# 32 bytes behind each 512-column block of the first half's operand tiles, and 96 bytes between the rings of high and low weight parts

## The chip, the cores and the metric

The kernel runs on one core of one Trainium2 chip. The metric is device time in microseconds of that core; lower is better.

## The reference

Two transformer-like blocks over a sequence of 1024 tokens with a width of 1024, in float32, one after the other.

```python
# first block
h = rmsnorm(x, g_mix); proj = h @ w_in            # q, k, v of three attentions, 3 gates
o_swa, o_dsa, o_mem = sliding window, top-256 sparse, memory cross attention
merged = sum(sigmoid(gate_i) * (o_i @ w_proj_i))
x = x + merged @ w_out
x = x + square(relu(rmsnorm(x, g_mlp) @ w_mlp_in)) @ w_mlp_out      # 4096 hidden
x = rmsnorm(x, g_final)
# second block, modulated by c: mod = silu(c) @ w_ada + b_ada
h = rmsnorm(x, g_mix_2) * (1 + sc1) + sh1
x = x + gt1 * mixer(h)                            # two-way mLSTM (4 heads) and pooling
h = rmsnorm(x, g_ffn_2) * (1 + sc2) + sh2
x = x + gt2 * (square(relu(h @ w_ff1)) @ w_ff2)
return rmsnorm(x, g_final_2)
```

## The kernel before, in words

Every large product is made of three matmuls in fp32r: each float32 operand is split in a high part (the value rounded to fp32r) and a low part (what is left), and hi x hi, hi x lo and lo x hi are accumulated in the same PSUM bank.

*Weights.* `wunit` (lines 135 to 138) takes a tile of high parts (`wh`) and one of low parts (`wl`) from two rings of three tiles each in the pool `wp`, and `wload` (128 to 133) lets SyncE load the float32 weights into a third ring (`wr`, two tiles), ScalarE round them into `wh` (L131) and VectorE or GpSimd write the rest to `wl` (L132). A tile of the rings has 4096 bytes in each partition, mostly eight blocks of 128 columns (512 bytes each). `gates_ahead` uses rings of its own (`fh`, `fl`, in the pool `fwp`) in the same way.

*Activations.* The 1024 tokens are worked in two halves (hf 0 and 1) of 512. `h_tiles` (152 and 153) makes, for one half, a tile of high and one of low parts, each with eight blocks (one for 128 of the 1024 features) of 512 columns, 2048 bytes to a block. The first half's tiles are in pool `hA`, the second half's in `hB`, or in `hBp` in the first block's MLP and in the second block's mixer. They are written block by block in `norm_turn` (L177, L178) and `make_h` (L1077 to L1081). The hidden layer of the MLPs (`hid_hi`, `hid_lo`, pool `hidp`), the merged product (`m_hi`, `m_lo`), the attention outputs (`o_s`, `om`, `od`) and the mixer's output (`y_s`) are held in the same way, in tiles of their own.

*The order on TensorE.* `gemm_T` (410 on) goes over the feature blocks c and, for each, over the halves. Each (c, half) is one trio: L419 streams the high part of the activations against the block of `wh`, L420 the low part against the same block, L421 the high part against the block of `wl`. `gemm2` (L1303 to L1305) and `gates_ahead` (L269 to L271) have the same trio. Each matmul has a weight load of its own, which runs while the matmul before it streams: beside L419 the `wh` block is loaded again (for L420), beside L420 the `wl` block (for L421), beside L421 the next `wh` block. Attention and the mLSTM use narrower matmuls and transposes; between these `fill` and `fill2` put single trios of the gates or projections. In `gemm_nat` (303 on) the roles are exchanged: the weights stream (256 to 384 columns) and 128 tokens of the activations are stationary.

*Where the tiles lie.* Pools on the left side of the memory grow upwards, those on the right side ("right") downwards from a fixed top; the tiles of a pool lie in ascending order of their first use. In each partition `h_hi` of `hA` begins at byte 21,728, its `h_lo` at 38,112, the pair of `hB` at 54,496 and 70,880, that of `hBp` at 88,032 and 104,416. `hid_hi` begins at 120,800 in the first MLP and 91,616 in the second. `wh` begins at 196,576, `wl` at 208,864, `wr` at 221,152 (it ends 32 bytes below the top of 229,376), and `fh` at 184,288. All of these are 224 more than a multiple of 256, and so are `m_hi`, `m_lo`, `y_s`, `o_s` and `od`. `om`, in a right-hand pool, begins at 161,632 and 169,824: 96 more than a multiple of 256. So do the tiles `m_hi` and `m_lo` of the memory's norm (pool `mT`, 145,504 and 153,696), which are stationary in `gemm_nat`. Three small unused tiles, `offA` (32 bytes), `offB` (768, before `hBp`) and `offC` (256, at the head of the second MLP's `hidp`) set some of these places.

Of the kernel before, what the change touches and what calls it, by code (L numbers as in the profile page):

```python
# [11 lines left out]
F32R = mybir.dt.float32r  # L12
# [7 lines left out]
P = 128  # L20
# [3 lines left out]
DC = D // P  # L24
# [36 lines left out]
def block_kernel(ctx, tc, x, mem, positions, g_mix, w_in, b_gate, sinks, g_mem, w_mem_kv, w_proj_swa, w_proj_dsa,  # L61
# [25 lines left out]
    def raw(ap):  # L87
        return ap.bitcast(F32)

    cst = Pool("cst")  # L90
    wp = Pool("wp", side="right")
# [33 lines left out]
        G.tensor_tensor(dst, dst, mhalf.to_broadcast(list(dst.shape)), op=OP.pow)  # L125


    def wload(src, k0, nk, c0, ncol, hi, lo, eng):
        r = wp([P, nk, ncol], F32, tag="wr", bufs=2)
        nc.sync.dma_start(r, src[k0 * P:(k0 + nk) * P, c0:c0 + ncol].rearrange("(k p) e -> p k e", p=P))  # L130
        A.copy(hi, r)  # L131
        (eng or V).tensor_tensor(lo, r, raw(hi), op=OP.subtract)  # L132
        return hi, lo

    def wunit(src, k0, nk, c0, ncol, eng=None):
        hi = wp([P, nk, ncol], F32R, tag="wh", bufs=3)
        lo = wp([P, nk, ncol], F32R, tag="wl", bufs=3)
        return wload(src, k0, nk, c0, ncol, hi, lo, eng)

# [9 lines left out]
    hA = Pool("hA")  # L149
    hB = Pool("hB")  # L150

    def h_tiles(pool):
        return tuple(pool([P, DC, 512], F32R, tag=f"h_{n}") for n in ("hi", "lo"))

    HT = [h_tiles(hA), h_tiles(hB)]

    def norm_load(pool, src, t):
# [87 lines left out]
    def gates_ahead(todo):  # L245
# [3 lines left out]
        def load(g, i):  # L249
            br, e = g  # L250
            hi = fwp([P, 4, P], F32R, tag="fh", bufs=2)
            lo = fwp([P, 4, P], F32R, tag="fl", bufs=2)
            units[g, i] = wload(w_in[0], 4 * i, 4, C_G + br * D + e * P, P, hi, lo, G)
# [61 lines left out]
    def nat_units(src, c0, ncol):  # L315
        if ncol <= P:
            return [wunit(src, 0, DC, c0, ncol)]
        return [wunit(src, 0, DC // 2, c0, ncol), wunit(src, DC // 2, DC // 2, c0, ncol)]
# [112 lines left out]
    def gate_tanh(br, e, put, eng=None):  # L431

        ug = [wunit(w_in[0], 0, DC, C_G + br * D + e * P, P, eng)]
        ag = [(hf, mm_bank()) for hf in range(2)]
        gemm_T(ag, ug, h_rhs)
        for hf, a in ag:
            A.activation(put(hf), a, AF.Tanh, bias=hbg[:, br * 8 + e:br * 8 + e + 1], scale=0.5)
# [421 lines left out]
    vd = kdp([P, NT, 64], tag="vd")  # L859
    ud = [wunit(w_in[0], k0, 2, C_QD, 384, G) for k0 in (0, 2)]  # L860
    ud += [wload(w_in[0], k0, 2, C_QD, 384, kdp([P, 2, 384], F32R), kdp([P, 2, 384], F32R), G) for k0 in (4, 6)]
    tr = Pool("tr")

# [220 lines left out]
    stp = Pool("stp", side="right")  # L1084
    xtp = Pool("xtp", side="right")
    HT[:] = [h_tiles(hA), None]
    xs = {}

# [19 lines left out]
    hBp = Pool("hBp")  # L1108
    hBp([P, 192], tag="offB")
    HT[1] = h_tiles(hBp)  # L1110


# [101 lines left out]
    hidp = Pool("hidp")  # L1214
# [494 lines left out]


    hidp = Pool("hidp")
    hidp([P, 64], tag="offC")
    ots = {}
    gb_ = hidp([P, D], tag="gb")
    nc.scalar.dma_start(gb_, g_final_2.unsqueeze(0).to_broadcast([P, D]))
# [68 lines left out]
```

## Time and profile before

| what | us |
|---|---|
| median of 2 runs | 2722.95 (2722.44 to 2723.46) |
| the profiled execution | 2722.59 |
| its span | 2720.9 |
| PE busy in the span | 2654.3 |
| VectorE / ScalarE / GpSimd busy | 1440.9 / 919.8 / 342.1 |

The span runs from the first to the last instruction of the program; 1.7 us of the execution lie around it. PE is TensorE. A matmul's record in the profile lasts longer than the step from its start to the next one's start, since matmuls are pipelined: at a step of 226 to 227 ns the record has 389 ns, and a step that is longer by some ns has a record that is longer by as many. The steps are read from the start times in the timeline.

### The profile page before, as it was taken

What the parts mean: (1) busy time and instruction counts of PE and PEld (TensorE: products, weight loads), DVE (VectorE), ACT (ScalarE), POOL (GpSimd) and SP (SyncE); (2) the same over time, 40 slices, a digit from 0 to 9 for tenths busy, and PEclk for the clock granted to TensorE, in tenths of its full rate; (3) what the DMA queues carried; (4) which work ended last, traced back from release to release, by engine and by line L of the source; (5) the groups of instructions that cost most, each with busy time, mean ns of one, the idle gap of its engine ahead of it and who ended that gap; (6) DMA issues with size and microseconds to landing.
All of it is one profiled execution on the core that took longest, in us unless ns stands there. A gap on an engine that the chain in (4) does not pass through costs nothing.

```text
span 2720.9 us, 34328 instructions
## 1 busy us (share of the span) xinstructions
PE 2654.3 (98%) x13328; PEld 2229.8 (82%) x13328; DVE 1440.9 (53%) x2836; ACT 919.8 (34%) x1826; POOL 342.1 (13%) x337
## 2 busy tenths in 40 slices
PE   7999999899999999999999989999999999999997
PEld 6899987788878888888888867888788888888886
DVE  7685878834455634553453476656553333333335
ACT  6575765335334221222212332332432122111223
POOL 3011123421001000000000331111310000000006
PEclk9999999999999999999999999999999999999999
DMA  3121122321154313331331124221421111121123
GB/s 114 53 61 40 31 75 88 93 57 41 63 166 124 108 46 114 116 100 52 108 101 55 57 55 151 63 78 39 139 70 54 57 37 47 51 58 48 39 62 124
DMA packets 263735, 206.41 MB, mean 76 GB/s; under 512 B 9468, under 2 KB 239636, under 8 KB 263572
## 3 DMA queue, kind: packets, MB, share of 16 engines
q1 hardware_dynamic: 255108, 180.25, 22.1%
q10 hardware_dynamic: 8464, 23.96, 2.6%
q8 instruction: 105, 1.72, 0.3%
q14 instruction: 58, 0.48, 0.1%
HBM read 185.24 MB, written 18.94 MB: 75 GB/s over the span
## 4 chain that ended last, share of the span: by engine, by line
PE 70%; DVE 4%; DMA 2%; ACT 1%; issue 1%; POOL 1%; POOLq 0%; SPq 0%; ACTq 0%; DVEq 0%
PE mm L420 19%; PE mm L421 19%; PE mm L419 19%; PE mm L1303 2%; PE mm L1305 2%; PE mm L1304 2%; PE tp L912 1%; DVE st_acc L1007 1%; PE mm L900 1%; DMA adaw<-in_w_ada_dram 1%; DVE h_lo L1081 0%; ACT wh L131 0%; DMA xt<-in_x_dram 0%; DVE t L1074 0%; PE fl L269 0%
## 5 line engine op out<-in xcount | busy, mean ns | idle before, releaser
L131 ACT CAST wh<-wr 128x1024 fp32r<-128x1024 f32 (+3 forms) x303 | 255.1, 843 | 689.2 <-PE mm L420 583.4
L421 PE MATMUL mm<-h_hi,wl 128*128 128x512 f32 x1248 | 486.1, 389 | 1.1 <-POOL wl L132 1.1
L419 PE MATMUL mm<-h_hi,wh 128*128 128x512 f32 x1248 | 486.5, 390 | 0.6 <-ACT ft L278 0.6
L420 PE MATMUL mm<-h_lo,wh 128*128 128x512 f32 x1248 | 485.7, 389 | 0.0
L420 PE MATMUL mm<-hid_lo,wh 128*128 128x512 f32 (+1 forms) x1056 | 405.5, 384 | 4.0 <-DVE hid_lo L1162 4.0
L419 PE MATMUL mm<-hid_hi,wh 128*128 128x512 f32 (+1 forms) x1056 | 407.4, 386 | 0.0
L421 PE MATMUL mm<-hid_hi,wl 128*128 128x512 f32 (+1 forms) x1056 | 405.1, 384 | 0.0
L132 POOL TENSOR_TENSOR wl<-wr,wh 128x1024 fp32r<-128x1024 f32 (+5 forms) x60 | 127.2, 2124 | 1466.8 <-ACT wh L131 1465.1
L1160 DVE TENSOR_TENSOR ml_q<-ml_r 128x512 f32<-128x512 f32 x128 | 88.1, 688 | 419.4 <-ACT ml_r L1158 419.4
L421 PEld LDWEIGHTS mm<-h_hi,wl 128*128 128x128 f32 x1248 | 234.4, 188 | 51.4 <-POOL wl L132 2.0
L419 PEld LDWEIGHTS mm<-h_hi,wh 128*128 128x128 f32 x1248 | 234.4, 188 | 49.7 <-ACT ft L278 0.8
L420 PEld LDWEIGHTS mm<-h_lo,wh 128*128 128x128 f32 x1248 | 234.5, 188 | 48.5
L132 DVE TENSOR_TENSOR wl<-wr,wh 128x1024 fp32r<-128x1024 f32 (+2 forms) x243 | 235.4, 969 | 52.0 <-ACT wh L131 48.5
L420 PEld LDWEIGHTS mm<-hid_lo,wh 128*128 128x128 f32 x1056 | 199.1, 189 | 43.8 <-DVE hid_lo L1162 5.5
L421 PEld LDWEIGHTS mm<-hid_hi,wl 128*128 128x128 f32 x1056 | 199.0, 188 | 39.0
L419 PEld LDWEIGHTS mm<-hid_hi,wh 128*128 128x128 f32 x1056 | 198.9, 188 | 38.5
L1158 ACT ACTIVATE ml_r<-mm 128x512 f32<-128x512 f32 x128 | 76.7, 599 | 449.2 <-PE mm L421 449.2
L1066 DVE SCALAR_TENSOR_TENSOR x<-mm,mod,x 128x512 f32<-128x512 f32 (+1 forms) x152 | 105.7, 722 | 223.0 <-PE mm L421 223.0
L1303 PE MATMUL mm<-h_hi,wh 128*128 128x512 f32 x320 | 131.8, 412 | 0.5 <-DVE kn L1336 0.5
L1305 PE MATMUL mm<-h_hi,wl 128*128 128x512 f32 x320 | 126.9, 396 | 3.3 <-DVE wl L132 3.3
L1304 PE MATMUL mm<-h_lo,wh 128*128 128x512 f32 x320 | 126.2, 394 | 0.0
L1064 DVE TENSOR_TENSOR h_hi<-mm,h_hi 128x512 f32<-128x512 f32 x72 | 49.6, 689 | 125.0 <-PE mm L421 124.9
(474 smaller groups left out, 4579.0 us busy)
## 6 DMA issues: line engine op xcount, KB each, us to landing
adaw<-in_w_ada_dram SPq DMA_DIRECT2D x48, 512.0 KB
wr<-in_w_ff_dram SPq DMA_DIRECT2D x44, 512.0 KB
wr<-in_w_in_dram SPq DMA_DIRECT2D x42, 512.0 KB
wr<-in_w_out_dram SPq DMA_DIRECT2D x32, 512.0 KB
wr<-in_w_mlp_in_dram SPq DMA_DIRECT2D x32, 512.0 KB
wr<-in_w_mlp_out_dram SPq DMA_DIRECT2D x56, 256.0 KB
wr<-in_w_ff_dram SPq DMA_DIRECT2D x56, 256.0 KB
wr<-in_w_in_dram SPq DMA_DIRECT2D x20, 256.0 KB
```

The lines of the kernel that those rows point to most:

```text
L131: A.copy(hi, r)
L132: (eng or V).tensor_tensor(lo, r, raw(hi), op=OP.subtract)
L419: mm(a, hi, r_hi, start=(i == 0), stop=False)
L420: mm(a, hi, r_lo, start=False, stop=False)
L421: mm(a, lo, r_hi, start=False, stop=(i == n - 1))
L1064: V.tensor_tensor(d, a, d, op=OP.add)
L1066: V.scalar_tensor_tensor(d, a, scale[:, e:e + 1], d, op0=OP.mult, op1=OP.add)
L1158: A.activation(r, a, AF.Relu)
L1160: V.tensor_tensor(q, r, r, op=OP.mult)
L1303: mm(a, hi[:, k, :], r_hi, start=(k == 0), stop=False)
L1304: mm(a, hi[:, k, :], r_lo, start=False, stop=False)
L1305: mm(a, lo[:, k, :], r_hi, start=False, stop=(k == DC - 1))
```

## The change

The tiles of `hA` get blocks of 520 instead of 512 columns; the last 8 (32 bytes) of each are never used. A tile of 24 floats (96 bytes) is put into the pool `wp` once, after the first `wh` and before the first `wl`. The 256 bytes of `offC` go.

```diff
+    off_w = []
...
     def wunit(src, k0, nk, c0, ncol, eng=None):
         hi = wp([P, nk, ncol], F32R, tag="wh", bufs=3)
+        if not off_w:
+            off_w.append(wp([P, 24], tag="offW"))
         lo = wp([P, nk, ncol], F32R, tag="wl", bufs=3)
...
     def h_tiles(pool):
-        return tuple(pool([P, DC, 512], F32R, tag=f"h_{n}") for n in ("hi", "lo"))
+        w = 520 if pool is hA else 512
+        return tuple(pool([P, DC, w], F32R, tag=f"h_{n}")[:, :, :512] for n in ("hi", "lo"))
...
     hidp = Pool("hidp")
-    hidp([P, 64], tag="offC")
```

By the layout above, block k of the first half then lies 32 k bytes further on, everything on the left behind `hA` 512 bytes further (256 in the second MLP's `hidp`), and `wh`, with every right-hand pool below `wp`, 96 bytes lower; `wl` and `wr` stay.

## Rows read from the trace of the kernel before

**Rows 1.** The page: busy time by engine, the granted TensorE clock in 40 slices of the span, and the shares of the chain that ended last, by engine and by line.

```profile
PE 2654.3 (98%) x13328; PEld 2229.8 (82%) x13328; DVE 1440.9 (53%) x2836; ACT 919.8 (34%) x1826; POOL 342.1 (13%) x337
...
PEclk9999999999999999999999999999999999999999
...
PE 70%; DVE 4%; DMA 2%; ACT 1%; issue 1%; POOL 1%; POOLq 0%; SPq 0%; ACTq 0%; DVEq 0%
PE mm L420 19%; PE mm L421 19%; PE mm L419 19%; PE mm L1303 2%; PE mm L1305 2%; PE mm L1304 2%; PE tp L912 1%; DVE st_acc L1007 1%; PE mm L900 1%; DMA adaw<-in_w_ada_dram 1%; DVE h_lo L1081 0%; ACT wh L131 0%; DMA xt<-in_x_dram 0%; DVE t L1074 0%; PE fl L269 0%
```

**Rows 2.** Two of the waits of PE for other engines, the first of the list and hid's: total us, times, longest.

```profile
PE tp L1024 <- DVE st_acc L1009: 7.4, 3, 3.8
...
PE mm L420 <- DVE hid_lo L1162: 4.0, 3, 1.7
```

**Rows 3.** Groups of the trio's first matmul with 512 columns, over the whole span, shapes apart: count | busy us, mean ns of a record | idle us before it.

```profile
L419 PE MATMUL mm<-h_hi,wh 128*128 128x512 f32 x1248 | 486.5, 390 | 0.6 <-ACT ft L278 0.6
L419 PE MATMUL mm<-hid_hi,wh 128*128 128x512 f32 x992 | 388.0, 391 | 0.0
L1303 PE MATMUL mm<-h_hi,wh 128*128 128x512 f32 x320 | 131.8, 412 | 0.5 <-DVE kn L1336 0.5
L269 PE MATMUL fl<-h_hi,fh 128*128 128x512 f32 x160 | 68.4, 427 | 1.4 <-ACT fh L131 1.0 <-ACT ft L278 0.4
L419 PE MATMUL mm<-m_hi,wh 128*128 128x512 f32 x128 | 51.6, 403 | 0.0
L419 PE MATMUL mm<-y_hi,wh 128*128 128x512 f32 x128 | 49.9, 392 | 1.3 <-ACT y_hi L1684 1.3
L419 PE MATMUL mm<-o_s,wh 128*128 128x512 f32 x64 | 25.0, 390 | 1.4 <-DVE gt L842 1.4
L419 PE MATMUL mm<-om,wh 128*128 128x512 f32 x32 | 13.9, 435 | 6.7 <-ACT gt L437 6.7
L419 PE MATMUL mm<-od,wh 128*128 128x512 f32 x32 | 12.4, 389 | 0.0
```

**Rows 4.** The stretch from 2100 to 2300 us, in the second MLP. First the busy us (and instructions) of PE, of its weight loads, of VectorE, ScalarE and GpSimd, the granted clock, the DMA share and GB/s; then two of the groups of matmuls in it.

```profile
2100.00:2300.00 200.00, 200.00 (x884) 165.68 (x883) 70.09 (x100) 41.48 (x67) 0.00 (x0) 1.00 0.16 47
...
L419 PE MATMUL mm<-h_hi,wh 128*128 128x512 f32 x167 | 65.0, 389 | 0.0
...
L420 PE MATMUL mm<-hid_lo,wh 128*128 128x512 f32 x128 | 49.8, 389 | 0.0
```

**Rows 5.** The timeline of PE in a long train of the first MLP: start us, length of the record in us, line and tiles. The first and the last of eight matmuls of the same kind that follow one another.

```profile
1089.66 0.39 PE L420 MATMUL mm<-h_lo,wh 128*128 128x512 f32 x1
...
1091.24 0.39 PE L421 MATMUL mm<-h_hi,wl 128*128 128x512 f32 x1
```

**Rows 6.** The stretch around 524 us: busy times and granted clock as in rows 4 (the clock is the third number from the end), then the first and the last of seven matmuls that follow one another.

```profile
522.70:525.60 2.90, 2.90 (x8) 2.31 (x7) 2.90 (x4) 0.45 (x1) 1.28 (x1) 0.50 0.00 0
...
522.71 0.63 PE L420 MATMUL mm<-om,wh 128*128 128x512 f32 x1
...
525.27 0.63 PE L420 MATMUL mm<-om,wh 128*128 128x512 f32 x1
```

**Rows 7.** The timeline of PE across one of om's products, at full clock: the first three of its twelve matmuls, and the one that follows the twelfth.

```profile
398.16 0.40 PE L419 MATMUL mm<-om,wh 128*128 128x512 f32 x1
398.40 0.39 PE L420 MATMUL mm<-om,wh 128*128 128x512 f32 x1
398.62 0.40 PE L421 MATMUL mm<-om,wl 128*128 128x512 f32 x1
...
400.95 0.39 PE L419 MATMUL mm<-h_hi,wh 128*128 128x512 f32 x1
```

**Rows 8.** The matmuls that stream om, over the whole span: min, median and max of a record in ns, first and last start.

```profile
L419 PE MATMUL mm<-om,wh x32: 390/395/793, 398.2 to 559.0; 128*128 128x512 f32 x32
L420 PE MATMUL mm<-om,wh x32: 387/394/628, 398.4 to 559.2; 128*128 128x512 f32 x32
L421 PE MATMUL mm<-om,wl x32: 392/396/628, 398.6 to 559.4; 128*128 128x512 f32 x32
```

**Rows 9.** The groups of `gemm_nat` with 256 columns: mean ns of a record after the bar. Here the weights stream and h or m is stationary.

```profile
L310 PE MATMUL mm<-wh,h_hi 128*128 128x256 f32 x256 | 74.2, 291 | 1.0 <-ACT vs L719 1.0
L311 PE MATMUL mm<-wl,h_hi 128*128 128x256 f32 x256 | 72.8, 285 | 0.6 <-DVE wl L132 0.5
L312 PE MATMUL mm<-wh,h_lo 128*128 128x256 f32 x256 | 72.5, 283 | 0.0
L312 PE MATMUL mm<-wh,m_lo 128*128 128x256 f32 x32 | 9.3, 292 | 0.0
L310 PE MATMUL mm<-wh,m_hi 128*128 128x256 f32 x32 | 9.1, 289 | 0.0
L311 PE MATMUL mm<-wl,m_hi 128*128 128x256 f32 x32 | 9.0, 283 | 0.0
```

**Rows 10.** VectorE's writing of h_lo in the second block's norms: min, median and max in ns.

```profile
L1081 DVE SCALAR_TENSOR_TENSOR h_lo<-t,mod,h_hi x32: 740/746/2578, 1584.4 to 2018.1; 128x512 fp32r<-128x512 f32 x32
```

**Rows 11.** The timeline of PE in the mixer, in a piece of twelve matmuls behind a small one of the mLSTM: the second, the seventh and the twelfth of them.

```profile
1751.24 0.39 PE L1304 MATMUL mm<-h_lo,wh 128*128 128x512 f32 x1
...
1752.40 0.39 PE L1303 MATMUL mm<-h_hi,wh 128*128 128x512 f32 x1
...
1753.54 0.39 PE L1305 MATMUL mm<-h_hi,wl 128*128 128x512 f32 x1
```

## The prediction

> **What bounds the kernel now.** I read the page first, then the waits of TensorE, then the matmul groups, then single matmuls in the timeline. The page shows a TensorE (PE) busy for 2654.3 us of a span of 2720.9 us, at full granted clock (2.4 GHz) in almost every slice, while VectorE is busy for 53% and ScalarE for 34% [rows 1]. The chain that ended last is PE for 70%, and its three big lines are the three products of the split matmul, L419 to L421 [rows 1]. PE's longest wait for another engine comes to 7.4 us in all [rows 2]. So the time is the number of PE's matmuls times the step from one start to the next. Of the matmuls, 512 columns wide and on the weight rings, there are 9312: three for each of 1248 (h), 992 (hid), 320 (h in the second half's projections), 160 (gates ahead), 128 (m), 128 (y), 64 (o_s), 32 (om) and 32 (od) [rows 3].
>
> The step is the thing to look at. In 2100 to 2300 us PE starts 884 matmuls in 200 us without idling, about 226.5 ns each, and its records there have a mean of 389 ns with h as with hid [rows 4]. One by one, seven steps from 1089.66 to 1091.24 us take 1.58 us, 226 ns each [rows 5]. 512 columns at 2.4 GHz are 213.3 ns, so about 13.3 ns come on top of each. Those 13.3 ns are no fixed work of the array: where the granted clock was at its lower level (1.2 GHz), six steps took 2.56 us, 427 ns each, and 512 columns at 1.2 GHz are 426.7 ns, nothing on top [rows 6]. I take the addition for the streaming operand (moving) and the next weights (stationary), read from the same memory at the same time.
>
> The rows also say that addresses matter. Before the change every moving tile of these groups and every weight block begins at the same place in 256 bytes (224 of 256), with one exception: om begins at 96, 128 bytes apart from the weights. There the twelve steps from 398.16 to 400.95 us take 2.79 us, 232.5 ns each, at full clock [rows 7], and the median records are 395, 394 and 396 ns against 389 ns [rows 8]. That is 6 ns more for the same instruction, lines and weights. With 256 columns no such price stands out: m against the weights (128 apart) has on L310 to L312 means of 289, 283 and 292 ns, h (0 apart) 291, 285 and 283 ns, so it is no dearer in two of three [rows 9].
>
> **The change part by part.** It adds and removes no instruction, DMA or wait; it moves tiles.
>
> *Blocks of the first half.* Block k of hA's tiles moves 32k bytes; 224 becomes 224, 0, 32 and so on through all eight places. hB, hBp and everything else on the left moves by 512 bytes, which leaves its place in 256 as it was.
>
> *The pad between the rings.* The pool of weights ends at a fixed top and lies in ascending order, so wl and wr stay and wh moves down by 96 bytes, to 128 of 256, and all right-hand pools with it. A matmul streams its operand while the weights of the next one load, and the order is hi with wh, lo with wh, hi with wl. So of three matmuls the first and third stream beside a load from wh, the second beside a load from wl. Where the moving tile is not padded (hB, hBp, hid, y, m, o_s) the distance becomes 96, 0, 96; in hA it is spread over all of 0 to 128.
>
> *offC.* Without it hid moves by 256 bytes net; its place in 256 stays. I cost this at nothing: the tile's waits are those on PE's own past reads, and PE's queue is in order. With no cover at all it would be hid's entry in PE's waits, 4.0 us now [rows 2].
>
> *Writers.* ScalarE and VectorE write the padded blocks one at a time, contiguous as before; I cost that at nothing. VectorE's 47% of idle time [rows 1] is the cover. A block's h_lo takes 746 ns at the median, and the second block's norms write 32 [rows 10]; without the cover, a tenth more on each would be 2.4 us.
>
> *Price of a distance.* The trace has distance 0 (389 ns) and 128 (395 ns on average), nothing between for 512 columns. Both ends for an unseen distance: the shortest record beside om is 387 ns [rows 8], -2 ns; the longest single steps beside om are 0.24 us [rows 7], some 11 ns above the step at distance 0. I take a straight line from 0 to +6 ns, as both known points lie on it: distance 96 costs 4.5 ns, and the eight places of hA, whose mean distance is 64, cost 3.0 ns on average.
>
> *The sum.* Long unbroken trains: h, hid, y and o_s, 2432 trios. Of them hA has half of h, 624 trios or 1872 matmuls at 3.0 ns: 5.6 us. The other 1808 trios have two matmuls each at 4.5 ns, 3616 in all: 16.3 us. Short trains, cut by attention and mLSTM work (320 + 160 + 128 trios): half of the first two is in hA, 720 matmuls at 3.0 ns, and 368 trios have two each at 4.5 ns, together 5.5 us. There the steps are already unsettled: from 1751.24 to 1752.40 us, after a small matmul, five steps took 232 ns each at distance 0, and the next five took 228 ns [rows 11]. So I count half, 2.7 us. om keeps 128 for most and od is too small to count. Total 24.6 us, on the profiled execution's 2722.59 us: 2747 us. That execution stands 0.4 us below the median of the runs shown (2722.95 us), so nothing is to be shifted.
>
> One rule of the Trainium skill speaks against all of this. Its page SBUF — State Buffer, section "Who interferes with whom", has it that the matmul's read port and the weight load's are independent and that PE never waits for anyone in the memory. By that rule placement costs nothing and the sum is 0; by the row on om it is the sum above, and the measurement of this kernel decides for me.
>
> **The rivals.**
>
> *A, nothing moves.* Perhaps only the distance 128 is bad, and the rest behaves as 0 does; or the settled step hangs on something else that om has. For it: 256-column matmuls show no clear price [rows 9]. Against it: om (395 ns) differs from o_s, whose mean is 390 ns [rows 3], by nothing but its place. Time: 2722.6 us. The rule quoted above would give this too.
>
> *B, faster.* In the long trains the new distances meet the weight loads less often than equal places do, and trains settle on a shorter step. Place: PE's steps in the two MLPs. Price: at the shortest record, 2 ns less for the 5488 matmuls that move in long trains, 11 us, so 2712 us; if the 13.3 ns went altogether for them, as at the lower clock, 73 us, so 2650 us. It decides from a mean step below 226.5 ns on. For it: the addition isn't the array's own [rows 6], and single short steps of 0.22 us occur beside om [rows 7]. Against it: they are followed by long ones, and the one other distance is dearer. The Trainium skill's page TensorE: Matmul & The Clock Gate, section "Wait — 56ns, not 53.3ns?", has 215.7 ns for back-to-back bf16 matmuls of 512 columns at full clock; if fp32r came to it in all 7296 matmuls of long trains, the time would be some 80 us less (an estimate from that page). No row here shows such a step.
>
> *C, no train settles.* The settled step needs equal places from matmul to matmul; with places that change at each, every matmul of the long trains goes at the unsettled step or om's, +6 ns, those at distance 0 too: 7296 x 6 ns = 44 us, so 2766 us; at om's longest step, +11 ns, 2803 us. For it: the trains need about six matmuls at equal places to settle [rows 11], and om never does in twelve. Against it: om's twelve do have equal places, so unequal ones are not what makes steps long.
>
> **How the numbers follow.** Forecast (24.6 us slower): 0.38; A 0.20; B 0.22, of which 0.07 beyond 2%; C 0.20, of which 0.11 beyond 2%; the forecast's own upper end gives another 0.02 there. A difference of 2% (54 us) is about what a measurement of this kernel can tell from no change: faster by more 0.07, slower by more 0.13, within 0.80. The forecast's own range is 2730 to 2766 us (half the price, up to C's first price). The range for 8 in 10 takes in A and B's small end and part of its large one, and C's up to the middle: 2692 to 2785 us. PE stays the bound in each case.
>
> **What would show it.** If I am right, the mean record of mm<-hid_hi,wh in the long trains rises from 389 to about 393 ns on L419 and L421, while L420 with hid_lo stays near 389 (its partner wl keeps distance 0), L419 to L421 with h rise by 3 to 4 ns, and PE starts some 870 matmuls instead of 884 in a 200 us stretch of an MLP. om's and the 256-column groups stay. PE's waits stay within a few us. C shows in L420 rising with the others; B in records below 389 ns; A in no change of either. I would be wrong in the premise if the steps were the same at every distance, and wrong in the sign if distance 96 were better than 0.

## The result and the profile after

The changed kernel takes 2758.8 us against 2722.95 us of the kernel before, two runs each: 1.0132 times as long, with an interval of 1.0088 to 1.0175. The forecast was 2747 us, 24.6 us more; 35.9 us more were measured, inside the range of 2692 to 2785 us and inside the forecast's own 2730 to 2766 us. In the later comparisons the kernel before has a median of 2722.0 us (seven runs), and 2723.0 and 2723.3 us in two single runs.

The profiled execution's span goes from 2720.9 to 2755.7 us. The page of after, with PE's two waits that answer to [rows 2]:

```profile
span 2755.7 us, 34328 instructions
...
PE 2689.1 (98%) x13328; PEld 2227.9 (81%) x13328; DVE 1443.0 (52%) x2836; ACT 918.2 (33%) x1826; POOL 342.1 (12%) x337
...
PE 71%; DVE 3%; DMA 2%; ACT 1%; issue 1%; POOL 1%; POOLq 0%; SPq 0%; ACTq 0%; DVEq 0%
PE mm L425 19%; PE mm L424 19%; PE mm L426 19%; PE mm L1308 3%; PE mm L1310 2%; PE mm L1309 2%; PE tp L917 1%; DVE st_acc L1012 1%; PE mm L905 1%; DMA adaw<-in_w_ada_dram 1%; ACT wh L133 0%; PE fl L274 0%; PE fl L276 0%; PE fl L275 0%; DMA wr<-in_w_ff_dram 0%
```

```profile
PE tp L1029 <- DVE st_acc L1014: 7.0, 3, 3.5
...
PE mm L425 <- DVE hid_lo L1167: 4.0, 3, 1.7
```

PE's busy time rises from 2654.3 to 2689.1 us, which is 34.8 us, and the span rises by 34.8 us as well. The number of instructions of every engine is that of [rows 1], VectorE and ScalarE stay within 2.1 us, PE's idle time is 66.6 us in both, and its waits for others are the old ones. So the whole loss lies in longer steps of the same matmuls. Lines of after stand some five numbers later than those of before: L424 to L426 are the trio L419 to L421, and L1308 is L1303. The groups that answer to [rows 3], here with all three lines for h and hid:

```profile
L424 PE MATMUL mm<-h_hi,wh 128*128 128x512 f32 x1248 | 491.9, 394 | 0.6 <-ACT ft L283 0.6
L425 PE MATMUL mm<-h_lo,wh 128*128 128x512 f32 x1248 | 491.8, 394 | 0.0
L426 PE MATMUL mm<-h_hi,wl 128*128 128x512 f32 x1248 | 491.6, 394 | 1.1 <-POOL wl L134 1.1
L424 PE MATMUL mm<-hid_hi,wh 128*128 128x512 f32 x992 | 392.2, 395 | 0.0
L425 PE MATMUL mm<-hid_lo,wh 128*128 128x512 f32 x992 | 390.7, 394 | 4.0 <-DVE hid_lo L1167 4.0
L426 PE MATMUL mm<-hid_hi,wl 128*128 128x512 f32 x992 | 389.6, 393 | 0.0
L1308 PE MATMUL mm<-h_hi,wh 128*128 128x512 f32 x320 | 132.9, 415 | 0.4 <-DVE kn L1341 0.4
L274 PE MATMUL fl<-h_hi,fh 128*128 128x512 f32 x160 | 68.5, 428 | 1.4 <-ACT fh L133 1.0 <-ACT ft L283 0.4
L424 PE MATMUL mm<-y_hi,wh 128*128 128x512 f32 x128 | 50.5, 397 | 1.3 <-ACT y_hi L1689 1.3
```

h gains 4 to 5 ns on each of its three lines and hid 3 to 4 ns: in the same view of before, whose first lines are [rows 3], h has 390, 389 and 389 ns and hid 391, 391 and 390 ns on L419, L420 and L421. The mixer's first line gains 3 ns and the gates ahead 1 ns. In a stretch of the second MLP, as in [rows 4]:

```profile
2150.00:2350.00 200.00, 200.00 (x866) 162.29 (x865) 72.53 (x102) 39.85 (x64) 0.00 (x0) 1.00 0.16 47
...
L424 PE MATMUL mm<-hid_hi,wh 128*128 128x512 f32 x156 | 61.5, 394 | 0.0
L425 PE MATMUL mm<-hid_lo,wh 128*128 128x512 f32 x156 | 61.3, 393 | 0.0
L426 PE MATMUL mm<-hid_hi,wl 128*128 128x512 f32 x156 | 61.2, 392 | 0.0
L425 PE MATMUL mm<-h_lo,wh 128*128 128x512 f32 x133 | 52.4, 394 | 0.0
L426 PE MATMUL mm<-h_hi,wl 128*128 128x512 f32 x133 | 52.3, 394 | 0.0
L424 PE MATMUL mm<-h_hi,wh 128*128 128x512 f32 x132 | 51.9, 393 | 0.0
```

The window counts 866 matmuls where there were 884. It also counts the records that reach into it from the left, and a record of 390 ns lasts 1.7 steps, so a step is 200 us by (count - 1.7): 226.7 ns before, 231.4 ns after. In the timeline, hid's steps in a settled train, the first and the last of thirteen matmuls that follow one another, beside [rows 5]:

```profile
2159.70 0.39 PE L426 MATMUL mm<-hid_hi,wl 128*128 128x512 f32 x1
...
2162.48 0.39 PE L426 MATMUL mm<-hid_hi,wl 128*128 128x512 f32 x1
```

Twelve steps in 2.78 us are 231.7 ns by these rounded starts. All three lines have them alike, which is the point where the prediction was off: L425, which streams beside a load from the wl ring at distance 0, is no cheaper than its neighbours. om, which lay 128 bytes from the weights before [rows 8], is now 128 or 32 bytes away, with medians 2 to 3 ns lower, and its longest L425 is the old 628 ns of the half-clock stretch [rows 6]:

```profile
L424 PE MATMUL mm<-om,wh x32: 390/393/796, 398.9 to 561.0; 128*128 128x512 f32 x32
L425 PE MATMUL mm<-om,wh x32: 390/392/628, 399.1 to 561.3; 128*128 128x512 f32 x32
L426 PE MATMUL mm<-om,wl x32: 392/393/628, 399.4 to 561.5; 128*128 128x512 f32 x32
```

### The profile page after: what moved, and what is told of

It is laid out like the page before. It is cut to its first block, busy times and chain, and to the rows that moved or that the text cites. A ratio compares the mean times of both kernels' runs of the same rounds, so it can differ in the third digit from the quotient of the medians.

```text
span 2755.7 us, 34328 instructions
## 1 busy us (share of the span) xinstructions
PE 2689.1 (98%) x13328; PEld 2227.9 (81%) x13328; DVE 1443.0 (52%) x2836; ACT 918.2 (33%) x1826; POOL 342.1 (12%) x337
## 4 chain that ended last, share of the span: by engine, by line
PE 71%; DVE 3%; DMA 2%; ACT 1%; issue 1%; POOL 1%; POOLq 0%; SPq 0%; ACTq 0%; DVEq 0%
PE mm L425 19%; PE mm L424 19%; PE mm L426 19%; PE mm L1308 3%; PE mm L1310 2%; PE mm L1309 2%; PE tp L917 1%; DVE st_acc L1012 1%; PE mm L905 1%; DMA adaw<-in_w_ada_dram 1%; ACT wh L133 0%; PE fl L274 0%; PE fl L276 0%; PE fl L275 0%; DMA wr<-in_w_ff_dram 0%
## 5 line engine op out<-in xcount | busy, mean ns | idle before, releaser
L426 PE MATMUL mm<-h_hi,wl 128*128 128x512 f32 x1248 | 491.6, 394 | 1.1 <-POOL wl L134 1.1
L424 PE MATMUL mm<-h_hi,wh 128*128 128x512 f32 x1248 | 491.9, 394 | 0.6 <-ACT ft L283 0.6
L425 PE MATMUL mm<-h_lo,wh 128*128 128x512 f32 x1248 | 491.8, 394 | 0.0
L425 PE MATMUL mm<-hid_lo,wh 128*128 128x512 f32 (+1 forms) x1056 | 408.7, 387 | 4.0 <-DVE hid_lo L1167 4.0
L424 PE MATMUL mm<-hid_hi,wh 128*128 128x512 f32 (+1 forms) x1056 | 411.5, 390 | 0.0
L426 PE MATMUL mm<-hid_hi,wl 128*128 128x512 f32 (+1 forms) x1056 | 407.6, 386 | 0.0
L426 PEld LDWEIGHTS mm<-h_hi,wl 128*128 128x128 f32 x1248 | 234.3, 188 | 57.2 <-POOL wl L134 2.0
L424 PEld LDWEIGHTS mm<-h_hi,wh 128*128 128x128 f32 x1248 | 234.4, 188 | 56.0 <-ACT ft L283 0.8
L425 PEld LDWEIGHTS mm<-h_lo,wh 128*128 128x128 f32 x1248 | 234.3, 188 | 54.7
L425 PEld LDWEIGHTS mm<-hid_lo,wh 128*128 128x128 f32 x1056 | 198.6, 188 | 47.3 <-DVE hid_lo L1167 5.4
L426 PEld LDWEIGHTS mm<-hid_hi,wl 128*128 128x128 f32 x1056 | 198.4, 188 | 44.2
L424 PEld LDWEIGHTS mm<-hid_hi,wh 128*128 128x128 f32 x1056 | 198.7, 188 | 41.7 <-ACT hid_hi L1166 0.2
L1308 PE MATMUL mm<-h_hi,wh 128*128 128x512 f32 x320 | 132.9, 415 | 0.4 <-DVE kn L1341 0.4
L1309 PE MATMUL mm<-h_lo,wh 128*128 128x512 f32 x320 | 126.9, 397 | 0.7 <-DVE h_lo L1086 0.7
```

The costliest lines, as they stand in the source:

```text
L424: mm(a, hi, r_hi, start=(i == 0), stop=False)
L425: mm(a, hi, r_lo, start=False, stop=False)
L426: mm(a, lo, r_hi, start=False, stop=(i == n - 1))
L1308: mm(a, hi[:, k, :], r_hi, start=(k == 0), stop=False)
L1309: mm(a, hi[:, k, :], r_lo, start=False, stop=False)
```

## The experiments

Each one is the kernel before with one edit. Times are medians; a single run is called one.

**Only the pad between the rings.**

```diff
     def wunit(...):
         hi = wp([P, nk, ncol], F32R, tag="wh", bufs=3)
+        if not off_w:
+            off_w.append(wp([P, 24], tag="offW"))
```

> Only the 96 bytes between the rings (offC stays, blocks of 512 columns). Theory P (each matmul has a price that goes by the distance between its own moving block and the weights loaded beside it): hid's trios as in the changed kernel, and now both halves of h at distances 96, 0, 96: all 7296 matmuls of long trains some 4.4 ns dearer, 32 us, so about 2755 us, and records of mm<-h near 393 to 394 ns on all three lines. Rival S (a train settles on the short step only where all three members of its trios have the same distance): the same 2755 us here. Rival N (the stride did it): 2723 us.

Measured: 2752.1 us, 1.0108 times the kernel before (1.0091 to 1.0125), 30 us more. The groups of its second MLP, 2150 to 2350 us (L423 to L425 are the trio here):

```profile
L423 PE MATMUL mm<-hid_hi,wh 128*128 128x512 f32 x161 | 63.4, 394 | 0.0
L424 PE MATMUL mm<-hid_lo,wh 128*128 128x512 f32 x161 | 63.3, 393 | 0.0
L425 PE MATMUL mm<-hid_hi,wl 128*128 128x512 f32 x161 | 63.2, 393 | 0.0
L423 PE MATMUL mm<-h_hi,wh 128*128 128x512 f32 x128 | 50.4, 394 | 0.0
L424 PE MATMUL mm<-h_lo,wh 128*128 128x512 f32 x128 | 50.3, 393 | 0.0
L425 PE MATMUL mm<-h_hi,wl 128*128 128x512 f32 x128 | 50.2, 392 | 0.0
```

h is now unpadded in both halves, and all lines have 392 to 394 ns, L424 at distance 0 among them. The pad alone makes five sixths of the change's loss. The size is what both theories said (2755 us) and doesn't tell them apart. The equal lines speak against a price for each matmul by itself: with such a price one of the three lines, the one at distance 0, would have stayed at 389 ns (the 393 to 394 ns on all three lines that were expected under P don't follow from it).

**Only the stride.**

```diff
     def h_tiles(pool):
+        w = 520 if pool is hA else 512
...
-    hidp([P, 64], tag="offC")
```

> Only the blocks of 520 columns in the first half's tiles, without offC. Theory P: only the matmuls that stream hA change, 1872 in long trains at 3 ns on average, 6 us, about 2729 us; the second half's steps and hid's stay at 226.7 ns (records of 389). Rival S: h's trains lose the settled step as a whole, 3744 matmuls at 4.4 ns, 16 us, about 2740 us, with records of 393 to 394 ns in both halves; hid stays at 389. Rival N: 2755 us.

Measured: 2742.5 us, 1.0074 times (1.0059 to 1.0089), 20.5 us more: theory P's 2729 us is out, S's 2740 us holds. The same stretch, in which both halves alternate trio by trio:

```profile
L422 PE MATMUL mm<-hid_hi,wl 128*128 128x512 f32 x164 | 63.8, 389 | 0.0
L420 PE MATMUL mm<-hid_hi,wh 128*128 128x512 f32 x164 | 63.8, 389 | 0.0
L421 PE MATMUL mm<-hid_lo,wh 128*128 128x512 f32 x163 | 63.4, 389 | 0.0
L420 PE MATMUL mm<-h_hi,wh 128*128 128x512 f32 x128 | 50.5, 395 | 0.0
L421 PE MATMUL mm<-h_lo,wh 128*128 128x512 f32 x128 | 50.5, 394 | 0.0
L422 PE MATMUL mm<-h_hi,wl 128*128 128x512 f32 x128 | 50.4, 394 | 0.0
```

hid, all at distance 0, keeps 389 ns. h has 394 to 395 ns on each line, a mean over the padded half and the other. That the unpadded half is dearer too beside the padded one shows if one finds it alone: at the head of an MLP three output tiles are worked for one half and then for the other, and from 2028 to 2042 us only the second half streams, unpadded:

```profile
L421 PE MATMUL mm<-h_lo,wh 128*128 128x512 f32 x21 | 8.2, 390 | 0.0
L420 PE MATMUL mm<-h_hi,wh 128*128 128x512 f32 x21 | 8.2, 389 | 0.0
L422 PE MATMUL mm<-h_hi,wl 128*128 128x512 f32 x21 | 8.2, 389 | 0.0
```

There the records are the old ones (389 to 390 ns), with the same tiles at the same places. If those matmuls kept 389 ns beside padded ones, the padded would need 399 to 400 ns for the mean of 394 to 395. Alone the padded ones don't take that. In this kernel's timeline a train of 24 matmuls on the padded half alone begins and ends so:

```profile
883.73 0.39 PE L420 MATMUL mm<-h_hi,wh 128*128 128x512 f32 x1
...
889.07 0.39 PE L422 MATMUL mm<-h_hi,wl 128*128 128x512 f32 x1
```

Its 23 steps take 5.34 us, 232.2 ns each, and its records are 0.39 to 0.40 us. The timeline says it directly, since of the two trios of each feature block the padded one comes first: by the start times, the h trains of the second MLP have steps of 232.9 ns on average where the moving tile is padded and 231.3 ns where it is not, against 226.7 ns for the unpadded half alone. So an unpadded matmul pays when its neighbours are padded.

**Only offC.**

```diff
-    hidp([P, 64], tag="offC")
```

> Only offC goes. All theories: the places in 256 bytes stay, 2723 us within 2 us, records of 389 ns for hid in the second MLP.

Measured: 2720.5 us, one run, with records of 389 to 391 ns in both MLPs, as before. offC costs and gives nothing that can be told here. The pad alone and the stride (with offC gone) alone come to 30 and 20.5 us, 50 us together; the whole change has 36 us. They don't add up: in the stretch from 2150 to 2350 us h has records of 392 to 394 ns with the one, 394 to 395 ns with the other and 393 to 394 ns with both, so its trains lose the short step only once.

**Both rings moved together: a constant distance.**

```diff
     def wload(...):
         r = wp([P, nk, ncol], F32, tag="wr", bufs=2)
+        if not off_w:
+            off_w.append(wp([P, 24], tag="offW"))
```

The pad (shown: 24 floats for 96 bytes; the others have a quarter of their bytes in floats) stands behind wr and moves wh and wl by the same bytes, and all right-hand pools with them; the moving tiles on the left stay. Every matmul that streams h, hid, m, o_s or y then has the same distance on all three lines. Two moving tiles lie on the right and go with the weights: om stays 128 bytes away from them, and od, which began at their place, stays at their place.

> A pad of 96 bytes behind the ring wr instead of between wh and wl, nothing else: both rings move down by 96 bytes together, so every matmul of the trios has distance 96, on all three lines. Theory P: all three lines pay the price of 96, 7296 x 4.5 ns = 33 us in the long trains, about 2756 us, records near 393 ns. Rival S: distances are equal again, trains settle at 226.7 ns, records of 389 ns, 2723 us.

Measured: 2770.7 us, 1.0174 times (1.0159 to 1.0189). Equal distances don't bring the short step back:

```profile
L425 PE MATMUL mm<-hid_hi,wl 128*128 128x512 f32 x139 | 55.5, 399 | 0.0
L424 PE MATMUL mm<-hid_lo,wh 128*128 128x512 f32 x140 | 55.2, 394 | 0.0
L423 PE MATMUL mm<-hid_hi,wh 128*128 128x512 f32 x140 | 54.9, 392 | 0.0
```

A distance of 96 costs more (392, 394 and 399 ns, a mean of 395) than the mixture of 96, 0 and 96 (393 ns). S, as it was put, falls: equality is not the condition. P's 2756 us is 15 us too low, and three lines at the same distance that differ by 7 ns don't fit a price that goes by a matmul's own distance.

> As with the 96 bytes behind wr, but 32: all distances are 32. Theory L (the straight line of the prediction, 0 at distance 0 and some 6.7 ns at 96 to 128): a fifth to a quarter of 6.7 ns, about 2734 us, records near 391 ns. Rival E (every unequal place costs the same, 6.7 ns): 2770 us, records near 396 ns. Rival W (one-sided: places just behind or ahead of each other are as good as equal ones, or better): 2723 us or less.

> The same with 64 bytes: all distances are 64. Theory L: about 3.3 to 4.5 ns, 2747 to 2755 us. Rival E: 2770 us. Rival W: 2723 us or less.

> The same with 128 bytes: all distances are 128, as om's was before; om itself lies at the weights' place again, since its pool moves too, at 128 from them. Theory L and rival E: steps near 233 ns, 2766 to 2772 us. Rival W leaves it open.

> The same with 192 bytes: 64 bytes apart on the other side. Theory L, if the price is symmetrical: as with 64, 2747 to 2755 us. Rival E: 2770 us. Rival W: better or worse than 64 by over 10 us, since what counts is which of the two runs ahead.

> Pad of 160 bytes behind wr: all distances are 160. So far the settled step in long trains is 226.7 ns at distance 0, some 229 at 64, and 233.3 at 32, 96, 128 and 192. Theory R (a settled trio lasts 680 ns or a whole number of 6.7 ns more, and 0 has the fewest): 229 to 233.3 ns, so 2735 to 2771 us; most likely the plateau, 2769 us. Rival L (straight line) would have 5 ns, 2756 us. Rival B (some distance beats 0): below 2722 us.

> The same with 224 bytes, 32 apart on the other side. Theory R: the plateau, as with 32 bytes, about 2769 us. Rival L: 1.5 ns, 2734 us. Rival B: below 2722 us.

> Pad of 256 bytes behind wr: all distances are 256 bytes more than before. If the place counts within 256 bytes, as the reading of the trace before has it, this is distance 0 again: 2722 us within 2 us, 884 matmuls in 200 us of an MLP. Rival: the period is longer (512 or more), or any move of the right-hand pools costs: 2735 to 2780 us as with the other pads.

One run each, except for 96, whose four runs are those above. The step is worked out from the count of the stretch from 2150 to 2350 us, as before. One matmul more or less in the count makes 0.3 ns; by the start times the steps of 32, 96, 128, 192 and 224 bytes are all 233.3 ns on average, and that of 160 is 234.3 ns:

| distance, bytes | us | matmuls in 200 us | step, ns |
|---|---|---|---|
| 0 (kernel before) | 2722.0 | 884 | 226.7 |
| 32 | 2770.7 | 859 | 233.3 |
| 64 | 2735.3 | 876 | 228.8 |
| 96 | 2770.7 | 859 | 233.3 |
| 128 | 2768.5 | 858 | 233.6 |
| 160 | 2780.3 | 855 | 234.4 |
| 192 | 2767.3 | 858 | 233.6 |
| 224 | 2765.8 | 859 | 233.3 |
| 256 | 2721.9 | 884 | 226.7 |

The rows of this stretch, with the columns of [rows 4], for 32, 64, 160, 224 and 256 bytes in this order:

```profile
2150.00:2350.00 200.00, 200.00 (x859) 160.62 (x858) 70.96 (x100) 40.01 (x65) 0.00 (x0) 1.00 0.16 46
```

```profile
2150.00:2350.00 200.00, 200.00 (x876) 164.09 (x875) 71.89 (x100) 38.20 (x60) 0.00 (x0) 1.00 0.18 51
```

```profile
2150.00:2350.00 200.00, 200.00 (x855) 160.79 (x854) 67.43 (x95) 39.55 (x65) 0.00 (x0) 1.00 0.15 44
```

```profile
2150.00:2350.00 200.00, 200.00 (x859) 161.02 (x858) 70.64 (x99) 39.24 (x63) 0.00 (x0) 1.00 0.15 45
```

```profile
2150.00:2350.00 200.00, 200.00 (x884) 165.62 (x883) 74.71 (x103) 39.83 (x61) 0.00 (x0) 1.00 0.19 54
```

There is no line: 32 bytes cost all that 128 cost, 64 a third of it. Theory L falls (its 2734 us for 32 bytes is 37 us too low, and for 224 bytes 32 us), and so does a symmetrical price (64 and 192 differ by 32 us). Rival E holds for six of the seven distances within about 10 us, but not for 64. Rival W, by which 32 and 64 bytes would be as good as 0 or better, falls with both; only its sign, a 192 that differs from 64 by over 10 us, came. Rival B found no distance that beats 0. The run at 256 is the control for all of them: every right-hand tile moved as in the others, and nothing changed, so it is the place within 256 bytes that counts and not the move. Nor do the other engines do more in such a stretch as PE gets slower: VectorE's column falls from 74.71 us at 256 to 67.43 us at 160, and ScalarE's stays between 38.20 and 40.01 us.

All these runs leave the moving tiles of h and hid at 224 of 256, so by them alone it could be the place 224 that counts, and not an equal place. od tells the two apart. In the run at 128 it lies with the weights at 96 of 256, and its median records are the old 389 ns (L424 has the median 389 too), while h and hid have means of 395 ns in the second MLP of that run:

```profile
L423 PE MATMUL mm<-od,wh x32: 389/389/397, 727.3 to 782.1; 128*128 128x512 f32 x32
L425 PE MATMUL mm<-od,wl x32: 389/389/397, 727.8 to 782.5; 128*128 128x512 f32 x32
```

Where only `wh` moved with od (the pad between the rings alone), its medians are 395, 393 and 394 ns.

The steps inside a train are not all alike, though every distance is the same. In the run at 64 each line keeps a step of its own, and one of them is shorter than at distance 0 (225.8 against 226.7 ns by the start times); in the run at 128 one line has short and long records (min, median and max in this stretch), and by the start times steps of 229 and 238 ns take turns:

```profile
L423 PE MATMUL mm<-hid_hi,wh 128*128 128x512 f32 x164 | 64.6, 394 | 0.0
L425 PE MATMUL mm<-hid_hi,wl 128*128 128x512 f32 x164 | 64.3, 392 | 0.0
L424 PE MATMUL mm<-hid_lo,wh 128*128 128x512 f32 x164 | 63.6, 388 | 0.0
```

```profile
L424 PE MATMUL mm<-hid_lo,wh x144: 392/395/398, 2159.9 to 2349.6; 128*128 128x512 f32 x144
```

So what goes by the distance is the length of the repeated pattern, and not each step in it.

**64 bytes between the rings.**

```diff
+            off_w.append(wp([P, 16], tag="offW"))   # between wh and wl
```

> 64 bytes between the rings instead of 96, nothing else: distances 64, 0, 64 in each trio. Theory P (each matmul pays for its own distance): two thirds of the price of 64, steps of 228.2 ns, about 2732 us. Theory R, by which the train settles as a whole: a trio of 680 or 686.7 ns, steps of 226.7 or 228.9 ns, 2723 or 2735 us. Rival B (a mixture meets the loads less often than equal places): below 2722 us.

Measured: 2739.8 us, one run.

```profile
2150.00:2350.00 200.00, 200.00 (x876) 164.08 (x875) 73.22 (x103) 38.81 (x61) 0.00 (x0) 1.00 0.17 50
```

876 matmuls in the stretch, the same as with 64 bytes everywhere: a step of 228.8 ns, where a price for each matmul would have given two thirds of the way, 228.1 ns or 879 matmuls. The whole time is 4.5 us above that of the constant 64, of which one run each says little: the four runs at 96 lie up to 4.8 us apart. So the members at distance 0 bring nothing: the train as a whole is as long as with 64 everywhere. Theory R's lengths fit as means for this one, 0, 64, the 96 mixture (693 ns a trio) and the 233.3 ns of most distances (700 ns), not for 160 (703 ns). Single trios don't fit it: by the start times trios of 695 and 705 ns alternate at 128, and at 160 the steps repeat after seven matmuls, 1640 ns. So the trio is not the unit in which a train settles.

## Why the prediction was right, and where it was not

*The bound and the place of the loss* were right. No instruction, DMA or wait came or went, PE stayed the bound, and busy time and span grew by the same 34.8 us, all of it in the 512-column trios. The 256-column groups of [rows 9] fell by 1 to 2 ns.

*That the price goes by the place within 256 bytes, of the moving tile against the weights,* was right: the run at 256 shows the one, od the other. It rested on one exception in the trace of before, om. The rule of the Trainium skill that was weighed against it (SBUF — State Buffer, "Who interferes with whom": PE never waits for anyone) gave 0 us; the runs give 36 us for this change and up to 57 us for a pad of 160 bytes (2780.3 us against 2723.0 us in the same comparison). The measurement decides.

*The price of a distance* was the term that was mis-sized. A straight line between 0 and 128 bytes gave 4.5 ns at 96 and 3.0 ns over the eight places of hA; that both known points lie on it was no evidence for it, since two points fix no shape. The runs have 6.6 ns at 96 and at nearly every other distance, and 2.1 ns at 64.

*The place of distance 0 in the sum* was wrong too. Every third matmul of the unpadded trios was put at nothing and the other two at 4.5 ns, 3.0 ns on average; measured are 3 to 4 ns on each line of hid, the L425 at distance 0 included, and 4.7 ns on the step of the second MLP (226.7 to 231.4 ns). The prediction had named L420 near 389 ns as its sign, and L420 rising with the others as that of rival C. The step of the prediction that failed is thus the price of each matmul by its own distance: the length of a train is made by all its members together. Of rival C the sign is seen, since the matmuls at distance 0 pay too, but not its mechanism. Trains do settle where places change (hid's steps at 96, 0, 96 are 230 to 232 ns, one like the other), and at a constant 96 they don't get the short step. C's price is not seen either: it put every train at +6 ns or more, and with 96, 0, 96 it is +4.4 to 4.7 ns. The two errors lean the same way, and the sum by the measured means shows it: h 1248 x (4 + 5 + 5) ns = 17.5 us, hid 992 x (4 + 3 + 3) ns = 9.9 us, y 1.7 us, the mixer's 320 trios 2.6 us, and m, o_s, od and the gates ahead 2.7 us, 34.4 us in all. Forecast were 21.9 us for the long trains, where h, hid, y and o_s have 29.9 us, and 2.7 us for the short ones, where 4.0 us are measured (m, mixer, gates).

The range of 2692 to 2785 us took in A and half of C as well, so that the time lies in it says little for the mechanism. A slip of the sum is small: `fl` moved together with `fh`, so that the third matmul of the gates ahead stood at 96 as well, 0.2 us by the prediction's own prices.

*Rivals.* A and B are out: no distance and no mixture that was tried is faster than equal places, and only 256 is as fast.

*offC and the writers* were rightly put at nothing: one run without offC has 2720.5 us, and VectorE and ScalarE are busy as before.

*Not settled.* That the moving stream and the weight load meet in the same part of the memory is an argument from the period of 256 bytes and from the half-clock stretch, where nothing came on top of the columns at distance 128 [rows 6]; no run took either stream away. Why 64 is cheap, why 32 is as dear as 128, and how a train carries its neighbours' places on from matmul to matmul stay open.

## What to carry to other kernels

Where one engine is busy for 98% and all its big instructions are of one kind, read the step from start to start and compare it between groups that differ in one thing; one odd tile (om) told that placement matters before anything was built. Keep the moving tiles and the weight blocks of fp32r trios at the same place within 256 bytes, and choose strides and pads as whole multiples of 256 bytes: a pad of 32 bytes that moves both rings costs as much as one of 128. Don't price unseen points on a line between two seen ones when matmuls may settle together; put the dearer end on all of them, and on their neighbours.

## What the runs showed that was not expected

A matmul's step depends on where its neighbours' tiles lie: the same unpadded trios have steps of 226.7 ns alone and 231.3 ns on average beside padded ones. The mean step of a long train falls into few values: 226.7 ns at equal places, 228.8 ns at 64 bytes, 231.1 to 231.4 ns at 96, 0, 96, and 233.3 to 234.4 ns elsewhere, while single steps in it may differ by 9 ns at one and the same distance. And 32 bytes of misplacement in an unchanged program cost 48.7 us, 1.8% of the whole.
